# Remaining columns of a weight through another queue, and earlier touches, in a QKV matmul on one core

## The chip, the core and the metric

The kernel runs on one NeuronCore of a Trainium2 chip. The metric is the device time of one execution in microseconds (us). The engines are named as in the profile: PE is TensorE (matmuls) with PEld its weight loads, DVE is VectorE, ACT is ScalarE, POOL is GpSimd, SP is SyncE, which only issues DMAs here.

## The reference

```python
def reference(x, w_qkv):                  # x 16x512x768, w_qkv 768x2304, float32
    qkv = np.matmul(x, w_qkv)             # 8192x768 by 768x2304
    q = qkv[..., :768]
    k = qkv[..., 768:1536]
    v = qkv[..., 1536:]
    return np.stack([q, k, v], axis=0)    # 3x16x512x768, float32
```

## The kernel before

x is taken as 8192 rows of 768 and worked on in 32 pairs, each of two tiles of 128 rows: pair p holds rows 256p to 256p + 255. The 2304 columns of w are cut into two blocks of 1024, called q = 0 and q = 1, and 256 remaining columns in the middle, at column 1024 (`R_OFF`).

From pair 2 on, a block of 256 rows by 1024 columns (a `quad`) is made with seven half-size products instead of eight, by sums of quarters of x and of w (`do(u, 1)` to `do(u, 7)`; `product`, L244, issues the matmuls). Products 1 and 2 take bfloat16 operands (`xb`, `b1`), the others the sums in a rounded float32 (`sr`, `ts`, `b22`). Product 6 accumulates onto the PSUM bank of product 1, after ScalarE has read that bank out (`evacuate`, L253). The remaining 256 columns are a plain bfloat16 product of `xb` and `w_rem` (`rem_row`, L299), two tiles of 128 rows to a bank, read out by ScalarE at L313 and stored by SyncE's queue.

Pairs 0 and 1, and both blocks of w, go through a start of their own. Its order is written out by hand, for each engine and queue; no scheduler moves anything. Each engine does its instructions in that order, and a waiting one holds up those behind it.

- SyncE's queue first loads the four tiles of 128 rows of pairs 0 and 1 (`load_row`, L163), then block q = 0 of w as float32 in slices of 128 x 512, the first in two half-width pieces (`load_slices`, L93), then pair 2 in eight loads of 96 KB, four for each half (`load_x_rows`, L138), then the two halves of the second block (`load_blocks`).
- ScalarE's queue issues two small loads, called `touch`, whose data is never read: 32 floats (128 bytes) of the first 128 rows that w's first slice reads, and of 128 rows of x, the third tile (rows 256 to 383).
- PE runs some matmuls of zeros (`busy`), turns the four tiles (`turn_row`), multiplies them with the slices of w as they come (`block`, L456), then does the remaining columns of pairs 0 and 1 (`rem`), then the first quad of pair 2 with the remaining columns of pair 2 in between, then the second block.
- VectorE casts the slices of w to bfloat16 (`cast_j`), forms the sums of w (`sum_w`, L120), and turns pair 2 in two halves (`transpose(2, 2)`, L154).
- ScalarE reads out banks of the first pairs (L446), does two casts, and rounds the two halves of pair 2 (`round_row`, L200), between which it reads out the bank of the remaining columns of pair 0 (L313) and two more banks.
- GpSimd waits until the first slice of the second half of w's block is there: `hold` copies one element of it into a `mark`, and so delays what stands behind it on GpSimd. Then it loads the remaining columns of w in two halves into the bfloat16 tiles `w_rem[0]` and `w_rem[1]` (L419); its DMA casts float32 to bfloat16 on the way. A second `hold` waits for the first half of pair 2, and GpSimd rounds a block of w.

```python
    hold(stage[0, 0, 1][:, 0, :1])
    for h in range(2):
        rows = w_qkv.rearrange("(p j) n -> p j n", j=KT)[:, h * KH:(h + 1) * KH]
        nc.gpsimd.dma_start(w_rem[h][:], rows[:, :, R_OFF:R_OFF + REM])
    hold(xin[2][:, 0, :1])
```

From pair 3 on the loop of `two(a, b, early)` does a quad of each block and the remaining columns for each pair, while the next pair is turned, rounded and summed by VectorE and GpSimd.

Names that the prediction uses: `st`/`stage` are the float32 slices of w, `both` a buffer that takes one half of the second block, `xin` the loaded rows of x, `xf` the turned ones, `o` the output tiles (`o_pool`, five buffers taken in turn), `orem` the output tile of the remaining columns, `ps` PSUM banks (eight in turn). L numbers are those of the kernel before; in the changed kernel lines from 404 on move by a few.

Of the kernel before, what the change touches and what calls it, by code (L numbers as in the profile page):

```python
# [10 lines left out]
def kernel(  # L11
# [20 lines left out]
    nc = tc.nc  # L32
    P = 128
    G = 32
# [4 lines left out]
    KT = K // P  # L39
    KH = KT // 2  # L40
# [3 lines left out]
    REM = N3 - 4 * CB  # L44
    Q_OFF = (0, 2 * CB + REM)
    R_OFF = 2 * CB
    fp32 = mybir.dt.float32
    f32r = mybir.dt.float32r
    bf16 = mybir.dt.bfloat16
    ident = mybir.ActivationFunctionType.Identity  # L50
# [3 lines left out]
    x_flat = x.rearrange("b t h -> (b t) h")  # L54
# [7 lines left out]
    o_pool = ctx.enter_context(tc.tile_pool(name="o", bufs=5))  # L62
# [4 lines left out]
    xb_pool = ctx.enter_context(tc.tile_pool(name="xb", bufs=4))  # L67
    rem_pool = ctx.enter_context(tc.tile_pool(name="rem", bufs=1))
    s_pool = ctx.enter_context(tc.tile_pool(name="s", bufs=2))
    m_pool = ctx.enter_context(tc.tile_pool(name="m", bufs=2))  # L70
    ps_pool = ctx.enter_context(tc.tile_pool(name="ps", bufs=8, space=bass.MemoryType.PSUM))


# [3 lines left out]
    w_rem = [w_pool.tile([P, KH, REM], bf16, name="w_rem0"), None]  # L77
# [13 lines left out]
    def load_w(dst, j0, nj, off, cols):  # L91
        rows = w_qkv.rearrange("(p j) n -> p j n", j=KT)
        nc.sync.dma_start(dst, rows[:, j0:j0 + nj, off:off + cols])  # L93

    stage = {}

    def load_slices(c, cuts):
        t = tq_pool.tile([P, KT, CB], fp32, name="st0", tag="tq")
        stage[0, 0, c], stage[0, 1, c] = t[:, :KH, :], t[:, KH:, :]
        for j, nj, lo, hi in cuts:  # L100
            load_w(t[:, j:j + nj, lo:hi], j, nj, Q_OFF[0] + c * CB + lo, hi - lo)
# [10 lines left out]
    def sum_w(q, n):  # L112
        t1, t2, t3, t4 = ts[q]
        o, in0, in1 = {
            1: (t1, stage[q, 0, 1], stage[q, 0, 0]),
            2: (t2, stage[q, 1, 1], t1),
            3: (t3, stage[q, 1, 1], stage[q, 0, 1]),
            4: (t4, stage[q, 1, 0], t2),
        }[n]
        nc.vector.tensor_tensor(o, in0, in1, op=sub)  # L120
# [10 lines left out]
    def load_x_rows(p, parts=range(8)):  # L131
        if p not in xin:
            xin[p] = xin_pool.tile([P, 2 * P // G, KC], fp32, name="xin")
        rows = x_flat[p * 2 * P:(p + 1) * 2 * P, :].rearrange("(g b) k -> b g k", b=G)
        for n in parts:
            r, i = divmod(n, 4)
            gs = slice(r * P // G, (r + 1) * P // G)
            nc.sync.dma_start(  # L138
                xin[p][i * G:(i + 1) * G, gs], rows[:, gs, i * KC:(i + 1) * KC]
            )  # L140
# [18 lines left out]
    def load_row(p, r):  # L159
        if r == 0:  # L160
            xin[p] = xin_pool.tile([P, 2, K], fp32, name="xin")
        row = (2 * p + r) * P
        nc.sync.dma_start(xin[p][:, r], x_flat[row:row + P, :])  # L163
# [29 lines left out]
    act, dve = nc.scalar, nc.vector  # L193
# [202 lines left out]
    zero = xb_pool.tile([P, CB], bf16, name="zero", tag="xb")  # L396
    nc.vector.memset(zero[:], 0.0)
    load_row(0, 0)
    touch = m_pool.tile([P, 2, G], fp32, name="touch")
    nc.scalar.dma_start(touch[:, 0], w_qkv.rearrange("(p j) n -> p j n", j=KT)[:, 0, :G])  # L400
    nc.scalar.dma_start(touch[:, 1], x_flat[2 * P:3 * P, :G])
    nc.scalar.activation(tiny[:], zero[:, :1], ident)
    make_identity(nc, eye)
    load_row(0, 1)
# [2 lines left out]
    half = CB // 2  # L407
    load_slices(0, [(0, 1, 0, half), (0, 1, half, CB)] + [(j, 1, 0, CB) for j in range(1, KT)])
    load_slices(1, [(j, 1, 0, CB) for j in range(KT)])
    load_x_rows(2)  # L410

    def hold(src):
        mark = m_pool.tile([P, 1], fp32, name="mark")
        nc.gpsimd.tensor_copy(out=mark[:], in_=src)  # L414

    hold(stage[0, 0, 1][:, 0, :1])
    for h in range(2):
        rows = w_qkv.rearrange("(p j) n -> p j n", j=KT)[:, h * KH:(h + 1) * KH]
        nc.gpsimd.dma_start(w_rem[h][:], rows[:, :, R_OFF:R_OFF + REM])  # L419
    hold(xin[2][:, 0, :1])  # L420
    load_blocks(1, 0)

# [6 lines left out]
    def cast_j(q, c, w, j, eng=act, n=slice(0, CB)):  # L429
        src = stage[q, j // KH, c][:, j % KH, n]  # L430
        if eng is act:
            eng.activation(w[:, j, n], src, ident)
        else:
            eng.tensor_copy(out=w[:, j, n], in_=src)
# [86 lines left out]
    cast_j(0, 1, bt, 3, dve)  # L521
    cast_j(0, 1, bt, 4, act)
    cast_j(0, 1, bt, 5, act)
    sum_w(0, 2)
    nc.gpsimd.tensor_copy(out=b22[0][:], in_=stage[0, 1, 1])
    late = block(
# [119 lines left out]
```

## Time and profile before

| what | us |
|---|---|
| median of three runs | 360.94 (360.82 to 362.36) |
| the profiled execution | 360.69 |
| its span, first to last instruction | 358.9 |
| PE busy in it | 352.3 |
| granted TensorE clock | 1.00 |

The profile tells of one execution. Its times count from the start of the span. Its page has the busy time of each engine and the chain of work that ended last; its timelines have the instructions in order of time, merged where they follow each other, with the idle time before them and what ended it in brackets (`<-`).

### The profile page before, as it was taken

How to read it: one execution, taken by the hardware profiler on the slowest of the kernel's cores; microseconds unless marked ns; L12 is line 12 of the kernel's file. 1: busy time of each engine (PE TensorE's matmuls, PEld its weight loads, DVE VectorE, ACT ScalarE, POOL GpSimd, SP SyncE). 2: the span in 40 equal slices, each digit the busy share in tenths (PEclk: the TensorE clock that was granted, in tenths of full speed). 3: DMA queues.
4: the chain of work that ended last, by engine and by line, in shares of the span. 5: the costliest groups of instructions: out<-in, count | busy, mean ns of one | idle time of the engine just before them, and what ended most of it. 6: DMA issues, size and time to landing. Idle time of an engine off the chain costs nothing.

```text
span 358.9 us, 5279 instructions
## 1 busy us (share of the span) xinstructions
PE 352.3 (98%) x1780; PEld 251.0 (70%) x1780; DVE 227.4 (63%) x244; ACT 185.7 (52%) x316; POOL 178.6 (50%) x187
## 2 busy tenths in 40 slices
PE   7999999999999999999999999999999999999995
PEld 3465577777777777777777777777777777777764
DVE  3879676676556675556676556676556676556643
ACT  5469644445444445444445544445545445545443
POOL 0221866435665444665444665444665444666420
PEclk9999999999999999999999999999999999999999
DMA  7999999798999999899999999988999899989767
GB/s 276 345 368 347 329 360 369 242 347 285 288 300 312 294 289 274 295 293 316 294 293 274 293 290 319 295 274 293 295 283 322 294 298 271 296 278 325 290 239 258
DMA packets 82106, 107.73 MB, mean 300 GB/s; under 512 B 5408, under 2 KB 62240, under 8 KB 82080
## 3 DMA queue, kind: packets, MB, share of 16 engines
q1 hardware_dynamic: 66672, 96.35, 82.4%
q10 hardware_dynamic: 14608, 10.65, 9.1%
q0 software_dynamic: 800, 0.39, 0.8%
q8 instruction: 14, 0.23, 0.3%
q14 instruction: 12, 0.10, 0.1%
HBM read 32.28 MB, written 75.50 MB: 300 GB/s over the span
## 4 chain that ended last, share of the span: by engine, by line
PE 92%; DMA 5%; ACT 1%; ACTq 0%; POOL 0%; SPq 0%; issue 0%
PE ps L244 78%; PE ps L299 11%; PE ps L456 3%; DMA w_rem<-in_w_qkv_dram 2%; DMA xin<-in_x_dram 1%; DMA st<-in_w_qkv_dram 1%; SPq L163 0%; ACT o L279 0%; ACTq L354 0%; POOL w_rem L419 0%; ACT orem L368 0%; POOL mark L414 0%; ACTq L370 0%; ACTq L368 0%
## 5 line engine op out<-in xcount | busy, mean ns | idle before, releaser
L244 PE MATMUL ps<-t,s 128*128 128x512 f32 x720 | 181.2, 399 | 0.0
L244 PEld LDWEIGHTS ps<-t,s 128*128 128x128 f32 x720 | 135.0, 188 | 30.7
L191 POOL CAST xb<-xf 128x1536 bf16<-128x1536 f32 x28 | 40.9, 1462 | 132.0 <-DVE xf L154 132.0
L276 DVE TENSOR_TENSOR o<-o,ps 128x512 f32<-128x512 f32 x58 | 39.9, 687 | 91.4 <-ACT o L275 91.4
L154 DVE STREAM_TRANSPOSE xf<-xin 128x1536 f32<-128x1536 f32 (+1 forms) x32 | 88.9, 2781 | 2.3 <-DMA xin<-in_x_dram 2.2
L244 PE MATMUL ps<-b,xb 128*128 128x512 bf16 x360 | 87.7, 380 | 0.0
L244 PEld LDWEIGHTS <-xb 128*128 128x128 bf16 x360 | 32.8, 98 | 37.3 <-issue 7.6
L269 ACT ACTIVATE o<-ps 128x512 f32<-128x512 f32 x60 | 35.9, 598 | 44.0 <-PE ps L244 41.3
L275 ACT ACTIVATE o<-ps 128x512 f32<-128x512 f32 x58 | 34.7, 598 | 44.3 <-PE ps L244 44.3
L282 DVE TENSOR_TENSOR o<-o,ps 128x512 f32<-128x512 f32 x60 | 41.2, 687 | 21.4 <-PE ps L244 20.2
L244 PE MATMUL ps<-b,s 128*128 128x512 f32 x180 | 50.4, 389 | 0.0
L279 ACT ACTIVATE o<-ps 128x512 f32<-128x512 f32 x60 | 35.9, 598 | 24.5 <-PE ps L244 21.6
L253 ACT ACTIVATE o<-ps 128x512 f32<-128x512 f32 x60 | 35.8, 597 | 24.4 <-DVE o L282 20.7
L299 PE MATMUL ps<-w_rem,xb 128*128 128x256 bf16 x384 | 47.5, 273 | 0.5 <-DMA w_rem<-in_w_qkv_dram 0.5
L299 PEld LDWEIGHTS <-xb 128*128 128x128 bf16 x384 | 37.2, 98 | 12.1 <-issue 1.4
L266 DVE TENSOR_TENSOR o<-o,ps 128x512 f32<-128x512 f32 x60 | 37.8, 672 | 2.0 <-ACT o L253 1.3
L244 PEld LDWEIGHTS ps<-b,s 128*128 128x128 f32 x180 | 33.8, 188 | 7.1
L212 POOL TENSOR_TENSOR s<-s,xf 128x384 fp32r<-128x384 f32 x29 | 29.4, 1013 | 2.3
L215 POOL TENSOR_TENSOR s<-xf,s 128x384 fp32r<-128x384 f32 x29 | 29.5, 1016 | 0.0
L213 POOL TENSOR_TENSOR s<-xf 128x384 fp32r<-128x384 f32 x29 | 29.4, 1013 | 0.0
L313 ACT ACTIVATE orem<-ps 128x512 f32<-128x512 f32 x31 | 18.5, 596 | 21.0 <-PE ps L299 21.0
L211 POOL TENSOR_TENSOR s<-xf 128x384 fp32r<-128x384 f32 x29 | 29.3, 1011 | 0.0
(45 smaller groups left out, 119.1 us busy)
## 6 DMA issues: line engine op xcount, KB each, us to landing
out_dram<-o SPq DMA_DIRECT2D x62, 768.0 KB, 4.9
out_dram<-o SPq DMA_DIRECT2D x65, 256.0 KB, 4.0
xin<-in_x_dram SPq DMA_DIRECT2D x62, 192.0 KB, 6.9
xin<-in_x_dram ACTq DMA_DIRECT2D x50, 192.0 KB, 4.2
out_dram<-orem SPq DMA_DIRECT2D x31, 256.0 KB, 5.8
st<-in_w_qkv_dram SPq DMA_DIRECT2D x11, 256.0 KB, 5.0
st<-in_w_qkv_dram SPq DMA_DIRECT2D x3, 768.0 KB, 10.1
xin<-in_x_dram SPq DMA_DIRECT2D x4, 384.0 KB, 4.3
```

Of the source, the lines that this page charges most:

```text
L154: nc.vector.transpose(turned[:, g:g + n], rows[:, g:g + n])
L191: nc.gpsimd.tensor_copy(out=xb[p][:], in_=xf[p][:])
L215: 4: lambda g: g.tensor_tensor(s[:, 4], a12, s[:, 2], op=sub),
L244: nc.tensor.matmul(ps[:], lhs[j], rhs[j], start=(start and j == 0), stop=(j == KH - 1), skip_group_check=True,)
L253: nc.scalar.activation(u.o[:, 0, :CB], u.x[:], ident)
L266: nc.vector.tensor_tensor(c11, c11, u.z[:], op=add)
L269: nc.scalar.activation(c12, u.x[:], ident)
L275: nc.scalar.activation(c22, u.x[:], ident)
L276: nc.vector.tensor_tensor(c22, c22, u.y[:], op=add)
L279: nc.scalar.activation(c21, u.x[:], ident)
L282: nc.vector.tensor_tensor(c12, c12, u.y[:], op=add)
L299: nc.tensor.matmul(ps, xb[p][:, j, r * P:(r + 1) * P], w_rem[j // KH][:, j % KH, :], start=(j == 0), stop=(j == KT - 1), skip_group_check= ...
```

## The change

The remaining columns of w are no longer loaded by GpSimd. SyncE's queue loads them as float32 into a staging tile `st_rem`, in two halves, behind the last slice of w's first block and ahead of pair 2 of x. ScalarE rounds each half to bfloat16, behind its two casts and ahead of two of its read-outs. GpSimd's first `hold` is gone. The staging tile takes a turn of the output tiles' buffers. The two touches change order and size: x first, now 128 bytes of each row of both tiles of pair 1 (256 rows, the third and fourth tile of x), then w as before. The pool of touches and marks has one buffer instead of two.

```diff
-    m_pool = ctx.enter_context(tc.tile_pool(name="m", bufs=2))
+    m_pool = ctx.enter_context(tc.tile_pool(name="m", bufs=1))
...
     load_row(0, 0)
-    touch = m_pool.tile([P, 2, G], fp32, name="touch")
-    nc.scalar.dma_start(touch[:, 0], w_qkv.rearrange("(p j) n -> p j n", j=KT)[:, 0, :G])
-    nc.scalar.dma_start(touch[:, 1], x_flat[2 * P:3 * P, :G])
+    touch = m_pool.tile([P, 3, G], fp32, name="touch")
+    nc.scalar.dma_start(touch[:, :2], x_flat[2 * P:4 * P, :G].rearrange("(t p) k -> p t k", t=2))
+    nc.scalar.dma_start(touch[:, 2], w_qkv.rearrange("(p j) n -> p j n", j=KT)[:, 0, :G])
...
     load_slices(1, [(j, 1, 0, CB) for j in range(KT)])
+    st_rem = o_pool.tile([P, KT, REM], fp32, name="str", tag="o")
+    for h in range(2):
+        load_w(st_rem[:, h * KH:(h + 1) * KH], h * KH, KH, R_OFF, REM)
     load_x_rows(2)
...
-    hold(stage[0, 0, 1][:, 0, :1])
-    for h in range(2):
-        rows = w_qkv.rearrange("(p j) n -> p j n", j=KT)[:, h * KH:(h + 1) * KH]
-        nc.gpsimd.dma_start(w_rem[h][:], rows[:, :, R_OFF:R_OFF + REM])
     hold(xin[2][:, 0, :1])
...
     cast_j(0, 1, bt, 5, act)
+    act.activation(w_rem[0][:], st_rem[:, :KH], ident)
+    act.activation(w_rem[1][:], st_rem[:, KH:], ident)
     sum_w(0, 2)
```

## The prediction

> **What bounds the kernel now.** I read the page first, then the chain that ended last, then the timelines of the engines between 12 and 28 us, and last the answers on the tiles xin, st, both and w_rem for when each transfer landed. The profiled execution took 360.69 us with a span of 358.9 us, so 1.8 us lie outside the span. It is 0.25 us under the median of the three runs, 360.94.
>
> From the page: the span, the engines' busy time, and the chain by engine.
>
> ```profile
> span 358.9 us, 5279 instructions
> ...
> PE 352.3 (98%) x1780; PEld 251.0 (70%) x1780; DVE 227.4 (63%) x244; ACT 185.7 (52%) x316; POOL 178.6 (50%) x187
> ...
> PE 92%; DMA 5%; ACT 1%; ACTq 0%; POOL 0%; SPq 0%; issue 0%
> ```
>
> PE is 92% of the chain; the 5% of DMA is all that loads can give back. The chain in order of time (start us, us, what) shows where it lies:
>
> ```profile
> 2.12 5.36 DMA xin<-in_x_dram
> ...
> 7.50 4.54 DMA st<-in_w_qkv_dram
> ...
> 12.09 0.44 POOL mark L414
> 12.53 0.86 POOL w_rem L419
> 13.38 6.39 DMA w_rem<-in_w_qkv_dram
> 19.78 0.04 issue
> 19.82 2.45 PE ps L299 x21
> ```
>
> From 19.82 us to 351.7 us the chain is PE alone. The mark (`hold`), the two GpSimd loads of w_rem and their landing at 19.78 us set when the remaining columns' matmuls (L299) can go on. That does not make 6.39 us the prize: the stall in PE's own timeline is.
>
> ```profile
> 18.85 0.49 PE L299 MATMUL ps<-w_rem,xb 128*128 128x256 bf16 x3
> 19.82 2.45 PE L299 MATMUL ps<-w_rem,xb 128*128 128x256 bf16 x21 [0.48 <-DMA w_rem<-in_w_qkv_dram]
> 22.11 1.46 PE L244 MATMUL ps<-b,xb 128*128 128x512 bf16 x6
> 23.41 1.47 PE L299 MATMUL ps<-w_rem,xb 128*128 128x256 bf16 x12
> 24.63 1.64 PE L244 MATMUL ps<-t,s 128*128 128x512 f32 x6
> ```
>
> Three matmuls on w_rem0 start at 18.85. One comes every 0.11 us (the 21 others take 19.82 to 22.11), so the fourth, the first on w_rem1, could start at 19.18. It starts at 19.82. The stall is **0.64 us**. The next work hangs on pair 2 of x (rows 512 to 767), which DVE turns and ACT rounds, in two halves:
>
> ```profile
> 17.58 1.60 DVE L154 STREAM_TRANSPOSE xf<-xin 128x768 f32<-128x768 f32 x1
> 20.85 1.57 DVE L154 STREAM_TRANSPOSE xf<-xin 128x768 f32<-128x768 f32 x1 [1.67 <-DMA xin<-in_x_dram]
> ```
>
> ```profile
> 19.22 0.84 ACT L200 ACTIVATE xb<-xf 128x768 bf16<-128x768 f32 x1 [0.86 <-DVE xf L154]
> 21.00 0.60 ACT L313 ACTIVATE orem<-ps 128x512 f32<-128x512 f32 x1 [0.94 <-PE ps L299]
> 21.49 1.08 ACT L446 ACTIVATE o<-ps 128x512 f32<-128x512 f32 x2
> 22.46 0.85 ACT L200 ACTIVATE xb<-xf 128x768 bf16<-128x768 f32 x1
> 23.21 0.58 ACT L313 ACTIVATE orem<-ps 128x512 f32<-128x512 f32 x1
> 23.68 0.60 ACT L253 ACTIVATE o<-ps 128x512 f32<-128x512 f32 x1
> ```
>
> ACT works without a pause from 21.00 to 24.28. Its last row here, L253, reads the bank that product 6 (PE at 24.63) accumulates into, so product 6 can't start before L253 ends. Now PE gets there at 24.61 and L253 is done 0.33 us before that.
>
> **The change, part by part.**
>
> *The GpSimd part goes.* The first `hold`, and two descriptor-writing issues of 0.92 and 0.78 us on POOL, are gone. POOL idles until 17.61 anyway (3.45 us before its second mark), so this saves nothing by itself. What it frees is transfer time: in the answer on DMA between 14 and 18.5 us the software queue has 740 packets at 60.3% of 16 engines, which is 59 ns for a packet of 512 bytes. Its 768 packets take 768 x 59 / 16 = 2.8 us of all engines. In the same stretch SP's queue falls behind.
>
> *The same columns as float32 on SP's queue, ahead of pair 2.* Two issues of 384 KB, in rows of 1 KB. The nearest rows are the two half-width slices of w, 128 KB each in rows of 1 KB: issued at 2.59 and 3.13, landing 5.2 and 5.1 us later, at 7.8 and 8.2, after the fourth x tile at 7.5. That is 0.36 us each, so 1.1 us for each half and 2.2 for both, against 2.8 for the software queue. The last undisturbed slice of w landed at 14.6 (9.46 + 5.2), slices come every 0.65 us (DVE's casts, which wait for them, start at 10.11, 10.82, 11.45, 12.06, 12.70 and 13.40), so the last one is in at 15.3, the halves of the remaining columns at **16.4** and **17.5**. The SP queue waits for a free semaphore before each issue (the eighth DMA before it); the issues behind stay 4 to 5 us ahead of their landings as now, so two more 0.4 us issues cost nothing as long as that lead lasts.
>
> *The two roundings on ACT.* Nearest row: L200, 128x768 float32 to bfloat16, 0.85 us. They stand behind the casts that end at 16.31 and ahead of two evacuations (L446, now 17.11 and 17.75). The first runs 16.4 to 17.3, the second 17.5 to 18.4, the evacuations end near 19.6. PE wants w_rem0 at 18.85 and w_rem1 at 19.18: in time by 0.8 us. Behind the waiting roundings stand only these evacuations, whose banks PE next needs for rem2 at 23.4, and L200, which waits for DVE. So the stall of 0.64 us goes, and PE could start product 6 at 24.63 - 0.64 = 23.99.
>
> *Pair 2 comes later, and this is what is late next.* Its eight loads of 96 KB stood behind the last slice; they now stand behind 768 KB more. The first half landed at 17.5 (the fourth load, issued 12.70, plus 4.8). Now it is 17.5 plus four loads: at 0.27 us (three quarters of a 128 KB load) 1.1 us, at the 0.35 us which separates its first two landings now (16.0 and 16.4, shared with the software queue) 1.4 us. So 18.6 to 18.9, and I take 18.7, as the software queue is gone. From landing to L200 on ACT is 1.74 us now (17.48 to 19.22): L200 starts at 20.45. From L200 on ACT is busy end to end; the spacings of its rows are 0.75 (L200 to L313), 0.49, 0.97 for the two L446, 0.75, 0.47, and L253's own 0.60: 4.03 us. L253 ends at 24.48, and product 6 starts some 0.05 later, at **24.53**. Against 24.63 that is a gain of 0.10 us, not of 0.64: ACT's row takes the place of the wait. The bounds 18.6 and 18.9 give 24.43 and 24.73, a gain of 0.2 or a loss of 0.1. The second half lands at 19.8 to 20.4 instead of 20.7, DVE turns it from 20.4, and its sum for product 6 is ready before 24; neither ends last. Behind pair 2 the blocks of w for q = 1 land earlier than now (23.3 for the first), so nothing later is short.
>
> *The touches.* They are two small ACT-queue loads, now 256 rows of x, then 128 of w, instead of 128 of each in the other order. Between 2 and 6 us that queue's 288 packets take 5.6% of 16 engines: 12 ns each. 128 more are 8 for each engine, **0.1 us** that every load of SP's queue behind them is later. What could be gained: the four x tiles land at 4.1, 5.1, 6.35 and 7.5, so the third and fourth take 1.25 and 1.15 us where the second takes 1.0; at 1.0 each it would be 0.4 us. But the third, which is touched now too, is the slowest. SP's third and fourth slice of w wait for the touches' semaphores (0.7 and 0.2 us) and would be issued a little later; their data is not due before 8.8. Ends: 0.1 lost, 0.4 gained, moving the start of the dense part (8.45 us) and pair 2 alike. I take 0, since the touched tile shows no gain and the touches now come earlier.
>
> *The buffers.* st_rem takes the first of five turns of the output tiles; the fifth quad waits for ACT's second rounding (18.4 us), long done when it is first written after 30 us. Cost nothing. m_pool's single buffer costs nothing, as each of its tiles is used once.
>
> **Sum.** 360.69 - 0.10 + 0 = 360.6 for a profiled execution; with the 0.25 us between it and the median, **360.8**. A change under 0.5% (1.8 us) is about what a measurement of this kernel can't tell from none.
>
> **Rivals.** *A, the gain arrives.* If pair 2's first half lands by 18.2, product 6 is set by PE at 23.99; with the touches' 0.4 it is up to 1.04 us, 359.9. For it: from the landing at 14.6 one slice (0.26 MB), the remaining columns (0.79 MB) and half of pair 2 (0.39 MB) are 1.44 MB, and at 404 GB/s, the best 2 us of this stage (12 to 14), they are in at 18.2. Against it: rows of 1 KB and 768 bytes moved more slowly than that. A typical size is 0.5 us, 360.4.
>
> *B, pair 2 is too late: slower.* One mechanism: the remaining columns in front of pair 2 hold up DVE's turn, L200 and so L253. It decides from a landing at 18.8 on, and from there costs its whole delay. If they take the software queue's 2.8 us instead of 2.2, the half lands at 19.3, product 6 starts at 25.13: 0.5 us slower, 361.4. If queue and pair move at the 223 GB/s of the stretch 16 to 18 us, 1.2 MB from 15.3 end at 20.6: 1.8 us slower, 362.7. Against it: that rate has the software queue in it. The Trainium skill ("DMA: Bandwidth & Descriptors", Issuing engines are not separate DMA queues) says that issuing from another engine saves the issue time only, the transfers sharing the same 16 engines; by that the data would take what it took, the 361.4 of this rival.
>
> *C, a cold PE.* In the first 3 us the warm-up matmuls come every 0.43 us, later 512-column ones every 0.22. Should a late x tile bring the slow rate back for some 3.4 us of the dense part, 1.7 us are lost: 362.5. PE's longest wait among the transposes is 0.56 us, and the touches move it by 0.1. The Trainium skill ("TensorE: Matmul & The Clock Gate", What's actually happening) has the slow clock return after an idle window of about 3.4 us, far more than any gap here.
>
> *D, something outside the span.* With no software queue in the program the 1.8 us outside the span might change; no row shows either sign.
>
> **How the numbers follow.** Forecast 0.52, with its own range 360.4 to 361.2 (pair 2's bounds, the touches' ends, 0.1 us of scatter); A 0.20; B 0.20, half of it under 361.5; C 0.03; D 0.05. 360.0 to 361.9 holds the forecast, nearly all of A, two thirds of B: 0.82. Faster by over 1.8 us needs D or what no row shows: 0.06. Slower by over 1.8 us is the end of B, C, and half of D: 0.10. Within: 0.84.
>
> **What would show it.** Right: L299 runs 24 matmuls from 18.85 with no DMA wait; ACT's second rounding ends before 18.8; the first turn starts near 18.8 instead of 17.58; PE waits for ACT's L253 (or L200) between 22 and 25 us; the chain names xin where it named w_rem. Wrong: a DMA wait at L299 still there, a first turn after 19.2 (then B), or product 6 at 24.0 (then A).

## The result: 0.19% slower, by product 6

The two kernels ran in turn on one chip, 14 executions each. The changed kernel's median is 361.97 us (361.36 to 362.43), that of the kernel before 361.14 (360.33 to 363.15): a ratio of **1.0019, 95% interval 1.0010 to 1.0028**. It is slower by 0.7 us (the ratio) to 0.8 us (the medians), where a gain of 0.1 us was forecast, and 361.97 lies 0.07 us above the predicted range of 360.0 to 361.9. The profiled execution took 361.69 us with a span of 359.9 (before 360.69 and 358.9).

From the page of the changed kernel: the span, the engines' busy time, the chain by engine.

```profile
span 359.9 us, 5248 instructions
...
PE 351.4 (98%) x1749; PEld 251.2 (70%) x1780; DVE 227.9 (63%) x244; ACT 187.1 (52%) x318; POOL 176.5 (49%) x184
...
PE 90%; DMA 5%; ACT 1%; issue 1%; ACTq 1%; DVE 0%; SPq 0%; DVEq 0%
```

The chain still has 5% of DMA in it. In order of time it now goes over pair 2 of x:

```profile
1.24 4.26 DMA touch<-in_w_qkv_dram
...
11.59 6.34 DMA str<-in_w_qkv_dram
...
17.94 3.96 DMA xin<-in_x_dram
...
22.02 1.59 DVE xf L154
...
23.63 0.84 ACT xb L200
24.47 0.48 ACT orem L313
24.96 0.50 ACT o L253
...
25.50 1.66 PE ps L244 x6
```

Where w_rem's landing released PE at 19.82, ACT's L253 now releases product 6, at 25.50 instead of 24.63. Two steps ahead of that stand the columns: pair 2's last load is issued at 17.94, the moment the second half of the columns (str) has landed. Further ahead stands the touch of w: SP's queue issues a slice of w behind it, at 5.52, so the chain alone doesn't clear the touches. PE's timeline has the gain and the loss side by side:

```profile
18.84 2.78 PE L299 MATMUL ps<-w_rem,xb 128*128 128x256 bf16 x24
...
24.53 0.83 PE L299 MATMUL ps<-w_rem,xb 128*128 128x256 bf16 x6 [0.45 <-ACT xb L200]
25.50 1.66 PE L244 MATMUL ps<-t,s 128*128 128x512 f32 x6
```

The 24 matmuls of L299 run without a pause: the stall of 0.64 us is gone, as forecast. Then PE waits for pair 2. Of DVE and ACT in the same stretch:

```profile
19.44 1.59 DVE L154 STREAM_TRANSPOSE xf<-xin 128x768 f32<-128x768 f32 x1 [1.80 <-DMA xin<-in_x_dram]
22.02 1.57 DVE L154 STREAM_TRANSPOSE xf<-xin 128x768 f32<-128x768 f32 x1 [0.99 <-DMA xin<-in_x_dram]
```

```profile
16.50 0.84 ACT L523 ACTIVATE w_rem<-str 128x768 bf16<-128x768 f32 x1 [0.20 <-DMA str<-in_w_qkv_dram]
17.95 0.84 ACT L524 ACTIVATE w_rem<-str 128x768 bf16<-128x768 f32 x1 [0.61 <-DMA str<-in_w_qkv_dram]
18.70 1.07 ACT L445 ACTIVATE o<-ps 128x512 f32<-128x512 f32 x2
21.06 0.84 ACT L200 ACTIVATE xb<-xf 128x768 bf16<-128x768 f32 x1 [1.30 <-DVE xf L154]
...
23.63 0.84 ACT L200 ACTIVATE xb<-xf 128x768 bf16<-128x768 f32 x1 [0.27 <-DVE xf L154]
24.38 0.58 ACT L313 ACTIVATE orem<-ps 128x512 f32<-128x512 f32 x1
24.86 0.59 ACT L253 ACTIVATE o<-ps 128x512 f32<-128x512 f32 x1
```

The first turn starts at 19.44 (before 17.58) and the first L200 at 21.06 (before 19.22). Both turns wait for xin. ACT has read out two banks by 19.77 and stands idle for 1.30 us before the first L200. ACT's second L200 waits for the second turn, so the second half counts too. The landings behind this, from the issues of the tiles: columns 16.47 and 17.93; pair 2's first half 19.42 (before 17.46), second half 21.90 (before 20.66).

From product 6 on, the two programs run in step: the span's end is 334.4 us behind it after and 334.3 before, and the last remaining-columns matmuls (L299) of the kernel start at 355.15 and 354.27. The whole difference is made before 25.5 us, and each experiment can be read at one point, the start of product 6. That start is also moved by the x tiles at the beginning (the dense part starts between 8.4 and 9.6 us, last section), so the distance from the dense start is given beside it: 16.18 us before, 17.06 after. That distance has a weakness too: a late x tile moves the dense start, and not always the landing on which product 6 hangs. The changed kernel with the new and with the old touches has product 6 at 25.50 and 25.47, but 17.06 and 16.47 behind the dense start. Neither column ranks kernels to half a microsecond; the ratios, over many executions, decide.

### The profile page after: what moved, and what is told of

Same layout as the page of the kernel before. It is cut to its first block, busy times and chain, and to the rows that moved or that the text cites. A ratio compares the mean times of both kernels' runs of the same rounds, so it can differ in the third digit from the quotient of the medians.

```text
span 359.9 us, 5248 instructions
## 1 busy us (share of the span) xinstructions
PE 351.4 (98%) x1749; PEld 251.2 (70%) x1780; DVE 227.9 (63%) x244; ACT 187.1 (52%) x318; POOL 176.5 (49%) x184
## 4 chain that ended last, share of the span: by engine, by line
PE 90%; DMA 5%; ACT 1%; issue 1%; ACTq 1%; DVE 0%; SPq 0%; DVEq 0%
PE ps L244 77%; PE ps L299 10%; PE ps L455 3%; DMA str<-in_w_qkv_dram 2%; DMA st<-in_w_qkv_dram 1%; DMA touch<-in_w_qkv_dram 1%; DMA xin<-in_x_dram 1%; DVE xf L154 0%; ACT o L279 0%; ACTq L354 0%; ACT xb L200 0%; SPq L93 0%; ACT orem L368 0%; ACT o L253 0%; ACTq L400 0%
## 5 line engine op out<-in xcount | busy, mean ns | idle before, releaser
L244 PE MATMUL ps<-b,xb 128*128 128x512 bf16 x331 | 85.3, 380 | 1.9 <-ACT xb L200 0.3
L253 ACT ACTIVATE o<-ps 128x512 f32<-128x512 f32 x60 | 35.8, 597 | 24.4 <-DVE o L282 20.7
L299 PE MATMUL ps<-w_rem,xb 128*128 128x256 bf16 x384 | 47.5, 273 | 0.4 <-ACT xb L200 0.4
L299 PEld LDWEIGHTS <-xb 128*128 128x128 bf16 x384 | 37.2, 98 | 12.2 <-issue 1.1
```

The source lines that it names most:

```text
L244: nc.tensor.matmul(ps[:], lhs[j], rhs[j], start=(start and j == 0), stop=(j == KH - 1), skip_group_check=True,)
L253: nc.scalar.activation(u.o[:, 0, :CB], u.x[:], ident)
L299: nc.tensor.matmul(ps, xb[p][:, j, r * P:(r + 1) * P], w_rem[j // KH][:, j % KH, :], start=(j == 0), stop=(j == KT - 1), skip_group_check= ...
```

## The experiments

Ratios are to the kernel before, timed in turn with it on the same chip, with 95% intervals. In the table, "product 6" is from the one profiled execution of each, "behind dense" its distance from the first matmul of `block` (the dense part; L456 in the kernel before).

| kernel | ratio | product 6 | behind dense |
|---|---|---|---|
| before | 1 | 24.63 | 16.18 |
| changed | 1.0019 (1.0010 to 1.0028) | 25.50 | 17.06 |
| half the columns' bytes | 1.0002 (0.9993 to 1.0011) | 25.70 | 16.19 |
| no bytes of the columns | 0.9985 (0.9974 to 0.9997) | 24.67 | 15.78 |
| roundings on GpSimd | 1.0037 (1.0023 to 1.0050) | 26.39 | 16.91 |
| changed, old touches | 1.0013 (1.0004 to 1.0022) | 25.47 | 16.47 |
| before, new touches | 1.0013 (1.0001 to 1.0024) | 25.58 | 16.76 |
| before, no touches | 1.0015 (1.0004 to 1.0027) | 25.98 | 16.59 |
| changed, pair 2 alternating | 1.0004 (0.9994 to 1.0014) | 25.34 | 16.34 |
| columns in one load | 1.0023 (1.0009 to 1.0037) | 25.34 | 16.61 |
| columns between the halves | 1.0011 (1.0000 to 1.0023) | 26.41 | 17.44 |
| columns on ScalarE's queue | 1.0037 (1.0024 to 1.0049) | 26.14 | 17.12 |
| the same, alternating | 1.0027 (1.0013 to 1.0041) | 26.27 | 17.00 |
| fetch earlier | 1.0041 (1.0025 to 1.0057) | 26.71 | 17.38 |
| changed, pair 2 into all partitions | 1.0185 (1.0169 to 1.0201) | 29.97 | 20.40 |
| before, pair 2 into all partitions | 1.0177 (1.0159 to 1.0195) | 30.65 | 21.89 |
| before, pair 2 alternating | 0.9991 (0.9979 to 1.0004) | 24.74 | 16.03 |
| before, mark one slice earlier | 0.9995 (0.9986 to 1.0004) | 25.57 | 16.68 |
| before, mark two slices earlier | 0.9997 (0.9988 to 1.0006) | 25.41 | 16.77 |
| before, mark one earlier, alternating | 0.9992 (0.9984 to 1.0001) | 24.72 | 16.01 |

**The theory** after the first comparison: the columns' 768 KB ahead of pair 2 on SP's queue make pair 2 late, as in rival B. **The rivals**: ScalarE's two roundings hold up its row; the touches did it.

**How many bytes.** Half of the columns loaded, and both roundings fed from it:

```diff
-    for h in range(2):
-        load_w(st_rem[:, h * KH:(h + 1) * KH], h * KH, KH, R_OFF, REM)
+    load_w(st_rem[:, :KH], 0, KH, R_OFF, REM)
...
-    act.activation(w_rem[1][:], st_rem[:, KH:], ident)
+    act.activation(w_rem[1][:], st_rem[:, :KH], ident)
```

> The changed kernel with only the first half of the remaining columns loaded (384 KB less on SP's queue); its rounding is done twice, so the second half of those columns' contraction uses wrong rows of w and that part of the output is left wrong. Theory (load order): pair 2 lands 1.1 to 1.5 us earlier (first half near 18.1), L253 ends near 23.9, product 6 starts at 23.9 to 24.3, 1.2 to 1.6 us earlier than in the changed kernel and 0.3 to 0.7 us earlier than before: ratio 0.998 to 0.9993. Rivals (touches, ScalarE's roundings): pair 2's landing moves, but product 6 stays at 25.0 or later, ratio 1.001 or more.

None of them loaded, the roundings reading slices that are in SBUF anyway:

```diff
-    st_rem = o_pool.tile([P, KT, REM], fp32, name="str", tag="o")
-    for h in range(2):
-        load_w(st_rem[:, h * KH:(h + 1) * KH], h * KH, KH, R_OFF, REM)
...
-    act.activation(w_rem[0][:], st_rem[:, :KH], ident)
-    act.activation(w_rem[1][:], st_rem[:, KH:], ident)
+    act.activation(w_rem[0][:], stage[0, 0, 0][:, :, :REM], ident)
+    act.activation(w_rem[1][:], stage[0, 1, 0][:, :, :REM], ident)
```

> The changed kernel with no load of the remaining columns at all: ScalarE's two roundings read the first 256 columns of slices that are in SBUF already, so those output columns hold other columns' products. Theory (bytes ahead of pair 2): pair 2's first half lands 2.2 to 2.8 us after the last slice of w and no stall is left before product 6, which starts 16.3 to 16.5 us after the dense part (24.63 less 0.64, less 0.18 to 0.34, measured from the first slice's matmuls, is 15.5; 16.2 in the kernel before); ratio to before 0.997 to 0.999, and against the half-bytes kernel another 0.2 to 0.6 us less. Rival (touches or ScalarE's roundings): ratio 1.000 or more.

Measured: 0, 384 and 768 KB ahead of pair 2 give 0.9985, 1.0002 and 1.0019, one step of 0.0017 or 0.6 us for each 384 KB. The middle interval overlaps both others; the two ends are clearly apart. The half was expected at 0.9980 to 0.9993 and gained less. The run without the bytes met its range of 0.997 to 0.999, with product 6 earlier behind the dense start than the 16.3 to 16.5 us expected. The touches are the same in all three, and the two roundings stand at the same place; without the bytes the staging tile is gone too, and the roundings wait for no load of their own. There, ACT's row from 20 us on is back to one without a wait for the second half:

```profile
20.11 0.84 ACT L200 ACTIVATE xb<-xf 128x768 bf16<-128x768 f32 x1 [0.35 <-DVE xf L154]
...
22.49 0.85 ACT L200 ACTIVATE xb<-xf 128x768 bf16<-128x768 f32 x1
...
23.70 0.62 ACT L253 ACTIVATE o<-ps 128x512 f32<-128x512 f32 x1
```

L253 ends at 24.32 there, with a dense start that was 0.44 us later than in the kernel before. So the load of the columns ahead of pair 2 is shown to be the cause, its bytes and the issue waits that it brings taken together. The 0.0015 that this kernel is faster than before, 0.5 us, is about the size of the removed stall; a kernel that computes these columns can't have it this way, as they have to be loaded.

**The roundings on GpSimd instead of ScalarE.**

```diff
+    nc.gpsimd.tensor_copy(out=w_rem[0][:], in_=st_rem[:, :KH])
+    nc.gpsimd.tensor_copy(out=w_rem[1][:], in_=st_rem[:, KH:])
     hold(xin[2][:, 0, :1])
...
-    act.activation(w_rem[0][:], st_rem[:, :KH], ident)
-    act.activation(w_rem[1][:], st_rem[:, KH:], ident)
```

> The changed kernel with the two roundings of the remaining columns on GpSimd instead of ScalarE, so that ScalarE has nothing new to do. Theory (load order): pair 2 lands as late as in the changed kernel (first half 19.2 to 19.6) and product 6 starts at 25.2 to 25.7, ratio to before 1.001 to 1.003. Rival (ScalarE's roundings hold up what stands behind them): product 6 moves to 24.0 to 24.7, ratio 0.998 to 1.000.

Slower, 1.0037, past both expectations. ACT, freed of both, waits all the longer for the turn:

```profile
22.33 0.84 ACT L200 ACTIVATE xb<-xf 128x768 bf16<-128x768 f32 x1 [2.98 <-DVE xf L154]
```

So ScalarE's roundings are not the cause; in the changed kernel, too, ACT waits 1.30 us for the turn after them. Why this kernel is slower than the changed one is not shown: in this execution the dense part also began 1.04 us later than in the changed kernel's.

**The touches.** The changed kernel with the touches of before, the kernel before with the new ones, and the kernel before without any:

```diff
-    touch = m_pool.tile([P, 3, G], fp32, name="touch")
-    nc.scalar.dma_start(touch[:, :2], x_flat[2 * P:4 * P, :G].rearrange("(t p) k -> p t k", t=2))
-    nc.scalar.dma_start(touch[:, 2], w_qkv.rearrange("(p j) n -> p j n", j=KT)[:, 0, :G])
+    touch = m_pool.tile([P, 2, G], fp32, name="touch")
+    nc.scalar.dma_start(touch[:, 0], w_qkv.rearrange("(p j) n -> p j n", j=KT)[:, 0, :G])
+    nc.scalar.dma_start(touch[:, 1], x_flat[2 * P:3 * P, :G])
```

> The changed kernel with the touches of before (w first, then 128 rows of x). Theory (load order: the remaining columns stand ahead of pair 2 in SP's queue): nothing of the 0.89 us comes back; product 6 still starts 0.7 to 1.1 us later than in the kernel before (25.3 to 25.7), ratio to before 1.0015 to 1.003. Rival (touches): the loads of SP's queue land 0.1 to 0.2 us earlier and the kernel is faster than the changed one by 0.1 to 0.4 us, ratio 1.000 to 1.001.

> The kernel before with the new touches alone. Theory (load order): nothing moves, ratio 0.9995 to 1.0005, w_rem lands at 19.6 to 20.0 and product 6 starts at 24.5 to 24.8. Rival (touches): pair 2 and w_rem land 0.1 to 0.3 us later and the ratio is 1.0005 to 1.002.

> The kernel before without any touch. Theory (the start's scatter is the chip's, and the touches do not change it): the fourth x tile lands at 7.3 to 8.6 us as in the profiles so far, and the ratio to before is 0.999 to 1.001. Rival (the touches spare a stall when the x tiles are first read): the fourth x tile lands later, 8.3 us or more, ratio 1.001 to 1.003. Other rival (touches only cost, so new ones cost more than old ones): ratio 0.998 to 0.9992.

On the changed kernel, old and new touches can't be told apart (1.0013 and 1.0019, intervals overlapping; 1.0013 falls between the two expectations); with the old ones it is still slower than the kernel before, so the touches are not needed for the loss. On the kernel before, the new touches cost 0.0013, where the theory expected nothing, and none at all 0.0015, as its first rival expected. Both intervals almost reach zero: the old touches seem worth about half a microsecond, and the new ones no more than none. How that adds to the columns stays unresolved: half a microsecond is the size of the scatter between executions at the start.

**Why pair 2 takes as long as it does.** Behind the columns its first half still takes 1.49 us (17.93 to 19.42), 0.37 for each load of 96 KB. Each load brings rows of 768 bytes into only 32 partitions. The order 0, 1, 2, 3 was turned into one in which neighbouring loads write groups in different halves of the 128 partitions:

```diff
-    load_x_rows(2)
+    load_x_rows(2, (0, 2, 1, 3, 4, 6, 5, 7))
```

> The changed kernel with the eight loads of pair 2 in another order: the quarters of the partitions 0, 2, 1, 3 instead of 0, 1, 2, 3, so that neighbouring loads go to different halves of SBUF's partitions. Theory (a load into 32 partitions alone moves at about half the rate, 50 to 60 ns for a 768-byte packet against 36): engines that have drifted apart work on both halves at once, the packets take 40 to 50 ns, pair 2's first half lands 0.2 to 0.5 us sooner after the columns' second half, and the kernel is 0.1 to 0.5 us faster than the changed one. Rival (pair 2 is late for its bytes or its issue alone): nothing moves, ratio to before 1.001 to 1.003 as in the changed kernel.

It gives 1.0004, lower than the changed kernel's 1.0019, but the intervals overlap. DMA queues of the changed kernel between 17 and 19 us (packets, MB, share of 16 engines), then of this one:

```profile
q1 hardware_dynamic: 756, 0.52, 109.8%
```

```profile
q1 hardware_dynamic: 839, 0.58, 103.2%
```

16 engines x 2 us x the share, over the packets, is 46 ns for a packet in the changed kernel and 39 ns in this one, the small packets that signal a landing included; the 768-byte packets alone take 51 and 43 ns. Same bytes, same sizes of packets, another order of partitions: some 15% faster a packet. The landings agree. By the ninth of the 16 engines to finish, which one late engine doesn't move, pair 2's first half is in 1.68 us behind the columns' second half in the changed kernel (17.23 to 18.91), and 1.34 us here; in the kernel before it is 1.77 us behind the last slice of w, and 1.41 with this order. The whole half is in at 19.61 all the same (19.42 in the changed kernel), as one engine was late here from the columns on. The Trainium skill ("SBUF — State Buffer", Door 1: The DMA port swizzle) says that the partitions of a transfer decide how many of 16 ports it reaches, and that a span of 32 reaches half of them; by that an estimate for a load is 98 KB at half of 435 GB/s, 0.45 us, and groups in different halves use different ports. The order's effect agrees in sign, and the measured 0.37 is better than the estimate. The Trainium skill ("SBUF — State Buffer", "Can I just issue two DMAs to hit both halves?") gives only 6% more from two such transfers at once; the 15% of the packets here are more than that, and what they are worth in time is not separated from the noise.

The direct test of the partitions was to cut the same bytes the other way, 32 rows into all 128 partitions (the edit cuts pair 3 so as well):

```diff
-        for n in parts:
-            r, i = divmod(n, 4)
-            gs = slice(r * P // G, (r + 1) * P // G)
-            nc.sync.dma_start(
-                xin[p][i * G:(i + 1) * G, gs], rows[:, gs, i * KC:(i + 1) * KC]
-            )
+        for g in range(8):
+            src = x_flat[p * 2 * P + g * G:p * 2 * P + (g + 1) * G, :]
+            nc.sync.dma_start(xin[p][:, g], src.rearrange("b (i k) -> i b k", k=KC))
```

> The changed kernel with pair 2's (and pair 3's) eight loads cut the other way: each brings 32 rows of x into all 128 partitions, where each brought one quarter of the columns of 128 rows into 32 partitions. Same bytes, same 768-byte packets, same number and order of issues. Theory 'partitions' (packets of 50 to 60 ns come from 16 engines writing into the same 32 partitions): packets take 36 to 40 ns, a half 1.15 us instead of 1.5, pair 2's first half about 10.6 us after the dense start (now 10.98), product 6 0.3 to 0.6 us earlier than in the changed kernel, ratio 1.0003 to 1.0012. Rival 'packet size' (768-byte packets have that price wherever they go): 50 to 60 ns, ratio 1.0019 as the changed kernel.

> The kernel before with pair 2's loads cut in that way. Theory 'partitions': the pair and the software queue beside it both get through sooner, w_rem lands 0.1 to 0.4 us earlier, the stall at L299 shrinks by as much, ratio 0.9988 to 0.9998. Rival 'packet size': ratio 1.000 within 0.0005.

Both missed widely: 1.0185 (1.0169 to 1.0201) and 1.0177 (1.0159 to 1.0195). DMA queue of the first between 18 and 20 us:

```profile
q1 hardware_dynamic: 253, 0.19, 27.9%
```

A packet takes 35 ns here (16 x 2 us x 0.279 / 253), but 27.9% of 16 engines is 4.5 engines: a load whose outer step counts four column blocks keeps only about four engines busy. So it says that a 768-byte packet can take 35 ns, and nothing on whether 16 engines get that rate into 128 partitions. In the first the clock fell as well: after PE had waited 1.34 and 2.79 us for pair 2, the granted clock was 0.61 between 30 and 32 us and 0.53 between 32 and 34. Partitions against packet size is supported by the order's effect and not settled by a direct test.

**Another queue, beside pair 2.** The columns issued from ScalarE's queue, behind a mark at the time of GpSimd's old one:

```diff
-    for h in range(2):
-        load_w(st_rem[:, h * KH:(h + 1) * KH], h * KH, KH, R_OFF, REM)
...
+    mark = m_pool.tile([P, 1], fp32, name="amark")
+    act.activation(mark[:], stage[0, 0, 1][:, 0, :1], ident)
+    for h in range(2):
+        rows = w_qkv.rearrange("(p j) n -> p j n", j=KT)[:, h * KH:(h + 1) * KH]
+        nc.scalar.dma_start(st_rem[:, h * KH:(h + 1) * KH], rows[:, :, R_OFF:R_OFF + REM])
     late0 = block(0, 0, b1[0], first)
```

> The columns as float32 as in the changed kernel, roundings on ScalarE kept, but issued from ScalarE's queue, behind a mark that waits for the first slice of w's second column block (12.1 us, where GpSimd's mark stood before). Pair 2 of x then stands on SP's queue right behind the last slice again, with the same 768 KB beside it and not ahead. Theory 'series' (768-byte packets into 32 partitions use the engines at half rate, the columns ahead of them are in series, and the loads wait for the columns' semaphores): pair 2's first half lands by 18.0, the columns by 18.6, no or a short wait at L299, product 6 at 24.0 to 24.6, ratio 0.998 to 1.000. Rival 'bytes only' (what counts is 768 KB more through the same 16 engines before the half is in, whatever the queue): first half at 19.0 to 19.5, product 6 at 25.1 to 25.5, ratio 1.0015 to 1.0025.

> As the run with the columns on ScalarE's queue, and pair 2's loads in the order 0, 2, 1, 3, 4, 6, 5, 7, so that neighbours write other partitions. Theory 'series': the columns beside the pair cover the half rate already, so the order is worth 0 to 0.2 us more, product 6 at 23.9 to 24.5, ratio 0.998 to 0.9995. Rival 'bytes only': the order changes nothing, same ratio as its neighbour, 1.0015 to 1.0025.

1.0037 and 1.0027: slower than the changed kernel or as slow, and past both expectations. In the first, the columns landed at 18.57 and 20.02, pair 2's first half at 20.24, and L299 waited again, 0.96 us for the second rounding. Between 16 and 18 us, the queues of the kernel before and then of the first of these:

```profile
q0 software_dynamic: 566, 0.28, 103.8%
q1 hardware_dynamic: 242, 0.16, 32.3%
```

```profile
q10 hardware_dynamic: 446, 0.44, 78.4%
q1 hardware_dynamic: 224, 0.15, 28.6%
```

GpSimd's queue and SP's together were at 136% of 16 engines, ScalarE's and SP's at 107%, which is no more than SP's queue reaches alone (109.8% above). A share over 100% means packets that are open at the same time on an engine, and a larger share is not a gain for SP's queue: beside the other it moved 0.16 and 0.15 MB in these 2 us, alone 0.52 MB. The Trainium skill ("DMA: Bandwidth & Descriptors", Issuing engines are not separate DMA queues) has all queues share the engines and says that a second one saves issue time only; the trace agrees, for the software queue too. So of the theory "in series" it is wrong that a queue beside pair 2 would cover it. A second cost shows in what SP's queue waits for at its issues. Between 14 and 21 us (us in total, times, longest), of the changed kernel and then of the first of these:

```profile
SPq L138 <- DMA str<-in_w_qkv_dram: 1.9, 2, 1.1
```

```profile
SPq L138 <- DMA str<-in_w_qkv_dram: 3.9, 2, 3.7
```

Pair 2's loads wait for landings of the columns, 1.9 us in all, though neither needs the other's data; with the columns on another queue the wait is longer still. In the changed kernel the seventh and eighth load are issued at 16.49 and 17.94, just behind the columns' 16.47 and 17.93.

**The issue waits alone.** The columns in one load, so that only one load of pair 2 waits for them:

```diff
-    for h in range(2):
-        load_w(st_rem[:, h * KH:(h + 1) * KH], h * KH, KH, R_OFF, REM)
+    load_w(st_rem[:], 0, KT, R_OFF, REM)
```

> The changed kernel with the remaining columns in one load of 768 KB instead of two of 384 KB, so that only pair 2's eighth load, not its seventh and eighth, is issued behind a landing of the columns. Theory 'issue waits' (they make the second half late, and L200's second row waits for it): the seventh load is issued near 16.0, the second half lands 0.3 to 0.7 us earlier or L200's second row no longer waits, product 6 0.1 to 0.3 us earlier, ratio 1.0010 to 1.0016; ScalarE's first rounding waits for the whole load, 17.9, which costs nothing as the second ended by 18.8. Rival 'bytes only': ratio 1.0019 as the changed kernel.

1.0023: no gain. The seventh load is issued at 15.56 and lands at 20.48, but the eighth is issued at 18.41 and lands at 21.62. In the profiled execution product 6 is 0.45 us nearer to the dense start than in the changed kernel, L200's second row not waiting; in the times this doesn't show. Against it stands a cost that was expected at nothing: ScalarE's roundings now wait for the whole load, until 18.42, and L299 stops again, its fourth matmul starting at 20.05 where 19.64 was possible. The waits' share is not separated from that of the bytes.

**The columns between the halves of pair 2.** With the old touches; the remaining columns' matmuls by halves of the contraction, the second half rounded by GpSimd (the loads alone are shown):

```diff
-    for h in range(2):
-        load_w(st_rem[:, h * KH:(h + 1) * KH], h * KH, KH, R_OFF, REM)
-    load_x_rows(2)
+    load_w(st_rem[:, :KH], 0, KH, R_OFF, REM)
+    load_x_rows(2, (0, 2, 1, 3))
+    load_w(st_rem[:, KH:], KH, KH, R_OFF, REM)
+    load_x_rows(2, (4, 6, 5, 7))
```

> A version meant to keep both: touches of before; SP's queue loads the first half of the columns, the first half of pair 2 (order 0, 2, 1, 3), the second half of the columns, the second half of pair 2; the remaining matmuls of pairs 0 and 1 do the first half of the contraction for all four tiles before the second; GpSimd rounds the second half; ScalarE reads product 1's bank before the second bank of the columns. Theory (product 6 is set by pair 2's landing through ScalarE's row): no stall at the columns, product 6 starts 0.3 to 0.7 us earlier after the dense part's start than in the kernel before, ratio 0.998 to 0.9993. Rival (the transfers of this stage are simply too many, whatever the order): product 6 no earlier than before, ratio 0.9995 to 1.002.

1.0011. The first half of pair 2 is early (18.91), the second, behind the columns' second half, lands at 23.14:

```profile
23.26 1.56 DVE L154 STREAM_TRANSPOSE xf<-xin 128x768 f32<-128x768 f32 x1 [2.65 <-DMA xin<-in_x_dram]
```

L200's second row waits 1.09 us for it. Part of that is one late engine, of the kind that the next paragraph looks at: the 15 others had brought their share by 21.63. PE also stops for 0.50 us at the columns, for GpSimd's rounding. The expectation failed, and its rival (0.9995 to 1.002) holds.

**A fetch of instructions.** In the changed kernel one packet of 16 KB (queue "instruction") takes 1.23 us of one DMA engine at 19.16, and one engine brings its part of pair 2's last two loads a microsecond later than the others (21.65 and 21.90, the next slowest 20.62 and 20.90). That it is the same engine is inferred from the time and the size, as the trace doesn't name it. The warm-up in more instructions moves it:

```diff
-    busy(8)
+    ps = bank()
+    for _ in range(32):
+        nc.tensor.matmul(ps[:, :P], zero[:, :P], zero[:, :P], start=True, stop=True)
```

> The changed kernel with the warm-up as 32 matmuls of 128 columns instead of 8 of 512 (the same columns, 48 more instructions on PE), so that the 16 KB fetch of instructions at 19.16 us comes some 5 us earlier. Theory 'the fetch made one engine late for the pair's seventh and eighth load': the second half lands by 21.0 instead of 21.90, L200's second row no longer waits for DVE, product 6 at 25.2 instead of 25.5, ratio 1.0008 to 1.0015. Rival 'one engine is late by the fetch wherever it falls, since all of them are busy from 9 us on': ratio 1.0019 as the changed kernel, product 6 at 25.4 to 25.8.

1.0041. The fetch came at 16.61, in the middle of the columns. One engine then finished the columns' first load at 18.66 (the next slowest 17.47), and both halves of pair 2 were late, 20.99 and 22.27, the second because its last load was issued at 20.24, behind the columns' landing at 20.23. Both expectations failed in size; the rival's account is nearer: an engine that is late stays late while its queue is full, wherever the fetch falls. Here it was worse, because the first half was hit too. Part of it is the start (0.89 us later), which this edit touches as well.

**A better version.** What the runs point to is the kernel before with pair 2 in the alternating order, without the columns on SP's queue; and the first mark on an earlier slice, so that GpSimd's loads start 0.65 or 1.3 us earlier:

```diff
-    load_x_rows(2)
+    load_x_rows(2, (0, 2, 1, 3, 4, 6, 5, 7))
...
-    hold(stage[0, 0, 1][:, 0, :1])
+    hold(stage[0, 1, 0][:, 2, :1])
```

The order alone, the earlier mark alone, the mark two slices earlier (`stage[0, 1, 0][:, 1, :1]`), and both edits shown:

> The kernel before with that order of pair 2's loads alone. Theory 'series': before, the software queue ran beside pair 2 and the stall at L299 (w_rem) set product 6; pair 2 lands 0 to 0.3 us earlier, w_rem as before at 19.5 to 19.9, product 6 at 24.4 to 24.7, ratio 0.9995 to 1.0005. Rival (the order itself is the gain that the alternating run showed over the changed kernel, 0.4 us): ratio 0.9985 to 0.9992.

> The kernel before with the first mark (hold) waiting for the sixth slice of w instead of the seventh, so that GpSimd's two loads of the remaining columns start 0.65 us earlier; nothing else moves. If the stall at L299 is the price to be had, and the software queue's packets run beside SP's on the same engines: w_rem lands near 19.2 instead of 19.8, the stall goes from 0.64 to about 0.1 us, pair 2's first half still lands by 17.8 and ScalarE's row does not take its place, product 6 near 24.1, ratio 0.9980 to 0.9992. Rival 'bytes ahead of pair 2' (whatever goes earlier makes slices and pair 2 later by as much): pair 2 0.3 us later and a wait of PE for a slice, ratio 0.9995 to 1.001.

> The same with the mark on the fifth slice, GpSimd's loads 1.3 us earlier. First account: w_rem near 18.5, no stall at L299, product 6 near 24.0, ratio 0.9978 to 0.9990. Rival: slices and pair 2 0.6 us later, ratio 1.000 to 1.002.

> The mark one slice earlier, and pair 2's loads in the order 0, 2, 1, 3, 4, 6, 5, 7. First account: as h1 or 0 to 0.2 us better, ratio 0.9975 to 0.9990. Rival: as h1's rival, the order changing nothing.

Measured: 0.9991, 0.9995, 0.9997 and 0.9992. All their intervals lie below the changed kernel's; none is shown to beat the kernel before. The order alone came out at its rival's range (0.9985 to 0.9992), but its interval holds 1 as well. The first account of the mark failed: GpSimd's first load was issued 3.39 us behind the dense start (12.28), 4.02 in the kernel before (12.47), but the second half of the columns landed at 20.71, not 19.2, and the wait at L299 stayed (0.61 us). With the mark two slices earlier it landed at 20.56, with one slice and the order at 19.87. In these executions, starting the columns earlier on a path that is full brought them no sooner.

## Why the prediction was wrong

- **The stall of 0.64 us goes: right.** L299 runs 24 matmuls from 18.84 in one piece. That this is not the prize, because ACT's row takes the wait's place, was right too.
- **The columns land at 16.4 and 17.5: the first is right (16.47), the second was forecast 0.43 us too early (17.93).** The 128 KB slices' price of 0.36 us held for the first half and not for the second (1.46 us for 384 KB by the last engine, 1.22 by the ninth of 16).
- **Pair 2's first half at 18.7, the step that failed.** It landed at 19.42, past the upper bound of 18.9 and past the 18.8 from which rival B was to decide. 0.43 of the 0.72 us are the columns' second half. The other 0.29 are the pair's own price: 0.30 us for a load was taken, 0.37 was measured. The sum took a value near the 0.27 scaled from loads of 1 KB rows, and its upper bound of 0.35 was the gap between pair 2's first two landings in the kernel before (16.04 and 16.39). The next two came at 16.93 and 17.46, gaps of 0.54 and 0.53: from the last slice's landing at 15.58, the four loads took 0.47 each beside the software queue. At that price the bound would have been 19.4. Without the software queue the price did fall, to 0.37 here and 0.34 in the run without the columns, but not to 0.30.
- **"The issues behind stay 4 to 5 us ahead": wrong for the last two loads.** They waited 1.9 us for landings of the columns; the second half landed at 21.90 where 19.8 to 20.4 was forecast. The prediction named the wait and took the lead for granted. The last microsecond of it is the one late engine: all others were done by 20.90, before the first turn ended at 21.03. Behind pair 2 the blocks of w for q = 1 came later, not earlier as forecast (the first at 23.66, before 23.33); the programs run in step from product 6 on all the same.
- **ACT's 4.03 us from L200 to L253's end: 4.39.** The row is the one named; 0.27 of the 0.36 more is L200's second row waiting for the second half, which the prediction had taken for done before. By the landings, this wait hangs on the one late engine.
- **The sum.** Product 6 came at 25.50, 0.97 behind the forecast 24.53: 0.61 at L200 and 0.36 from there on. The remaining 0.2 us between 360.8 and 361.97 is the median itself, 361.14 here and 360.94 in the runs that the sum began with. That the two add up so well is luck in part, as product 6 is from one execution. A change under 0.5% was said to be hard to tell from none; with 14 executions of each kernel the interval was 0.09% to either side.
- **Roundings and buffers at nothing: right** as far as the runs show. Taking the roundings from ScalarE did not help.
- **The touches at nothing (0.4 gained to 0.1 lost): not confirmed.** Alone on the kernel before they cost 0.04 to 0.87 us. With the old touches the changed kernel is still slower than before (1.0013), so they are not the whole of it. Their part in the change is open.
- **The rivals.** B is what happened, and its price lies between its two cases (0.5 and 1.8 us). A's gain came only with no bytes ahead of pair 2 (0.9985). C and D did not occur: the granted clock was 1.00 and 1.8 us lie outside the span in both. C's slow clock was seen in the run that brought pair 2 into all partitions, behind a wait of 2.79 us.

## What to carry to other kernels

A wait that is removed by moving its data onto another queue is paid by what stands behind on that queue: find that row's slack first, and price it with all of its own landings in the trace, not with the best pair of them; where the slack is smaller than the spread, take the bad end. Count the issues too, since a load may wait for landings of earlier ones, whoever's they are. In a full stage, look at the last engine of a load as well as at the middle one. Differences of half a microsecond should be read at a point behind which the programs run in step, against many executions.

## What the runs showed of the hardware

- **The start scatters.** The fourth tile of x landed at 7.48 us (before), 7.46 (changed) and up to 8.59 in the other kernels, most of whose edits lie after it; the ninth of 16 engines was done by 7.0 to 7.7, and one or a few were late. The dense part began between 8.44 and 9.57. The two profiled executions that the prediction and the first comparison rest on were both early ones.
- **A full queue keeps an engine's lateness.** In the changed kernel one engine is 1.03 and 1.00 us behind the next at pair 2's last two loads, and still 0.9 us behind at the three loads of w after them. Fetches of 16 KB took 0.9 to 1.4 us of one engine; that a fetch makes the late engine is inferred.
- **A queue beside SP's takes from it.** With GpSimd's both stood at 136% of 16 engines, with ScalarE's at 107%; SP's moved 0.16 and 0.15 MB of it in 2 us, and 0.52 MB alone at 110%.
- **The order of loads into groups of 32 partitions sets the price of a packet.** 768-byte packets took 51 ns in the order 0, 1, 2, 3 and 43 ns in the order 0, 2, 1, 3.
- **How a load is cut decides how many engines carry it.** 96 KB as 32 partitions by 4 rows used all 16; as 4 column blocks by 32 rows, 4.5.
- **The clock fell behind one wait and not behind another.** In the changed kernel with pair 2 into all partitions PE waited 2.79 us up to 29.00, and the granted clock was 0.61 and then 0.53 between 30 and 34; in the kernel before with the same cut it waited 2.55 us, and the clock stayed at 1.00.
